# A two-stream transformer layer on one core: norm statistics, delta keys and queries, and triangular blocks of the mixer's front computed in another form

## The chip, the cores and the metric

The kernel runs on one core of a Trainium2 chip. The metric is the device time of one execution in microseconds (us). Five engines of the core work side by side, each through its own queue in a fixed order: PE (matrix products and transposes), DVE (vector operations), ACT (scalar functions, through tables), POOL (vector operations too) and SP (which here only issues DMAs).

## The reference, cut to what matters

One layer over two streams, 1024 latent tokens and 256 context tokens of width 1024, all in fp32: a half step of a gated feed-forward (inner width 2816), a mixer, another half step for the latent tokens, and a last norm. Scales and shifts of the norms come from a conditioning vector through `w_mod`. The mixer has one input projection (`w_in`) and two groups of heads: four of a gated delta rule, run in both directions, and four of attention with norms and rotary embedding.

```python
qkv = silu(centred_dwconv(p[..., :1536], conv_w))            # 5 taps over tokens
q, k, v = split(qkv, 3)
q = l2norm(q per head of 128); k = l2norm(k per head of 128) # x * rsqrt(sum x*x + EPS)
...
kb = k * beta
a_mat = where(strict, (kb @ k^T) * decay, 0)                 # per chunk of 64 tokens
u = triangular_solve(a_mat + eye, v * beta); w = triangular_solve(a_mat + eye, kb * exp(gcum))
...                                                          # scan over chunks: o
out_delta = rmsnorm(o, gain) * silu(z)
aq = rope(rmsnorm(q_attn, q_norm)); ak = rope(rmsnorm(k_attn, k_norm))
```

## The kernel before

Order of the work, with the times at which each part runs in the profiled execution: a start (to 45.6) that turns the context and computes the first modulation columns from `w_mod`; the context loop (to 257.0), eleven steps `g` of up to three products with `ffn_w` in split precision, with side work handed in between by a table (`todo`, L830); the latent half step (a class `HalfStep`, whose steps are drawn from a generator `hs1.stream`); the mixer's second norm with the first projections of v and z (L749, L755); the mixer's front (977.5 to 1424.8); attention together with the delta rule's scan; the output projection, the second half step and the final norm.

In the *front* each projection is a product of the normed activations with a slice of `w_in`, whose fp32 weights are split into a high and a low half (`whi` on ACT, `wlo` on POOL or DVE). Then:

- `conv_head` (L1070) takes a head of k, q or v through five taps. The first tap is on ACT, four are on DVE (`ac<-pp,cols,ac`). Silu is a tanh on ACT and a product on DVE (`ac<-pp,ac`). Then PE transposes `ac` to token rows (L1105) and DVE copies them to `tk` (L1110). For k and q, ACT sums squares, DVE makes a reciprocal root of the sums (`rsq`, L1018: two integer steps, three rounds of three), POOL multiplies `tk` by it, PE transposes back (L1124), ACT copies, and a DMA stores the result in `kT_d` or `qT_d`. It is a generator that stops once, before POOL's product; `pump` and `late` resume it a head later.
- `rope_out` (L1034) does the same for one chunk of 128 tokens and two attention heads: a copy and two sums of squares on ACT, twelve small DVE steps, two DVE products, and for latent chunks four POOL steps.
- `stage1` (L1233) makes the strictly triangular blocks of two directions for one of ten chunks: products on PE into `psD`, an exponential on ACT, masks on POOL, products on DVE (`s1N`), transposes (L1258), stores into `nb_d`.
- `invert` (L1268) inverts the 32x32 diagonal blocks, by forward substitution, in three batches of 128, 128 and 64 blocks, one block per partition: two DVE steps (`tmb`, `Xb`) for each of 31 columns, then a DVE copy `Lb` (L1282) and two stores. Batches follow their chunks: four, four and two calls of `stage1`, then one `invert`.
- The last stage (from about 1366) runs the last 256 columns of the attention's q and of z, chunk by chunk, while `stage2_load` (L1306) has SP read the blocks back into `slot` tiles.

A scheduler sets the order on each engine when the program is built: each engine's queue is fixed, and steps of different places stand interleaved in it, roughly in the order of the program.

## Time and profile before

| | us |
|---|---|
| median of 3 runs | 2517.65 |
| lowest, highest run | 2512.27, 2519.01 |
| profiled execution | 2513.8 |
| its span | 2512.0 |
| busy in it: PE, DVE, ACT, POOL | 2353.8, 1884.6, 1129.3, 879.0 |

The mean granted clock of the profiled execution is 0.975. Over the whole span PE is busy 94% of the time and DVE 75%, but these shares are averages over stages of different kinds. The chain of work that ended last puts 52% of the span on PE and 21% on DVE. So what a change in one stage is worth is read from the table by stretches and from PE's waits in that stretch.

### The profile page before, as it was taken

What the parts mean: (1) busy time and instruction counts of PE and PEld (TensorE: products, weight loads), DVE (VectorE), ACT (ScalarE), POOL (GpSimd) and SP (SyncE); (2) the same over time, 40 slices, a digit from 0 to 9 for tenths busy, and PEclk for the clock granted to TensorE, in tenths of its full rate; (3) what the DMA queues carried; (4) which work ended last, traced back from release to release, by engine and by line L of the source; (5) the groups of instructions that cost most, each with busy time, mean ns of one, the idle gap of its engine ahead of it and who ended that gap; (6) DMA issues with size and microseconds to landing.
All of it is one profiled execution on the core that took longest, in us unless ns stands there. A gap on an engine that the chain in (4) does not pass through costs nothing.

```text
span 2512.0 us, 36679 instructions
## 1 busy us (share of the span) xinstructions
PE 2353.8 (94%) x12877; PEld 2004.7 (80%) x12877; DVE 1884.6 (75%) x3354; ACT 1129.3 (45%) x2355; POOL 879.0 (35%) x734
## 2 busy tenths in 40 slices
PE   8999999999989998988787899998999999999998
PEld 5999887877778878866676799887877888877887
DVE  4779768988798864677999766798488456667886
ACT  4575533332233454354443365566274334223445
POOL 0000243545532333345522534531034444663320
PEclk9999999999999999989898999999999999999999
DMA  8966425465684433324422545532333324446432
GB/s 299 303 205 220 163 101 168 143 209 202 203 278 138 139 134 100 91 60 131 125 83 83 152 115 180 171 101 108 119 101 126 126 106 155 151 160 217 139 126 84
DMA packets 345111, 377.86 MB, mean 150 GB/s; under 512 B 73707, under 2 KB 249503, under 8 KB 344543
## 3 DMA queue, kind: packets, MB, share of 16 engines
q1 hardware_dynamic: 311856, 328.16, 40.3%
q10 hardware_dynamic: 33071, 47.36, 5.8%
q8 instruction: 102, 1.67, 0.3%
q14 instruction: 82, 0.67, 0.1%
HBM read 283.41 MB, written 92.01 MB: 149 GB/s over the span
## 4 chain that ended last, share of the span: by engine, by line
PE 52%; DVE 21%; issue 8%; DMA 7%; POOL 6%; ACT 5%; SPq 1%; ACTq 0%; DVEq 0%; POOLq 0%
PE psw L407 28%; PE pd L55 7%; PE psA L55 6%; DVE ac L52 3%; DVE macc L52 3%; DVE ulo L49 2%; PE psw L55 2%; PE po L55 2%; DMA wr<-in_ffn_w 2%; PE pS L55 1%; DMA R<-gda 1%; PE psB L55 1%; PE psY L860 1%; DVE k L49 1%; DVE tmb L49 1%
## 5 line engine op out<-in xcount | busy, mean ns | idle before, releaser
L407 PE MATMUL psw<-xo,uhi 128*128 128x512 f32 x1536 | 492.7, 398 | 32.2 <-DVE k L49 15.6
L407 PEld LDWEIGHTS psw<-xo,uhi 128*128 128x128 f32 x1536 | 295.5, 192 | 100.0 <-ACT k L46 14.1
L407 PE MATMUL psw<-slot,uhi 128*128 128x512 f32 x1024 | 319.8, 390 | 5.1 <-DVE nk L49 3.0
L407 PE MATMUL psw<-xo,ulo 128*128 128x512 f32 x768 | 304.5, 396 | 0.0
L49 DVE TENSOR_TENSOR ulo<-wr,uhi 128x512 fp32r<-128x512 f32 (+1 forms) x272 | 215.1, 813 | 67.5 <-ACT uhi L46 64.4
L49 POOL TENSOR_TENSOR R<-wr 128x512 f32<-128x512 f32 (+1 forms) x68 | 95.4, 1413 | 391.0 <-DMA wr<-in_ffn_w 348.9
L407 PEld LDWEIGHTS psw<-slot,uhi 128*128 128x128 f32 x1024 | 192.2, 188 | 46.7 <-issue 3.8
L46 ACT ACTIVATE uhi<-wr 128x512 fp32r<-128x512 f32 (+1 forms) x272 | 150.8, 597 | 128.3 <-PE psw L407 68.3
L407 PE MATMUL psw<-slot,ulo 128*128 128x512 f32 x512 | 199.2, 389 | 0.0
L407 PEld LDWEIGHTS psw<-xo,ulo 128*128 128x128 f32 x768 | 148.0, 193 | 30.6
L55 PE MATMUL psA<-hc,whi 128*128 128x256 f32 x832 | 155.7, 285 | 1.8 <-ACT sil L46 1.8
L52 DVE SCALAR_TENSOR_TENSOR macc<-wv,cs,macc 128x512 f32<-128x512 f32 x140 | 135.6, 987 | 17.4 <-DMA wv<-in_w_mod 16.3
L46 ACT ACTIVATE whi<-wr 128x1024 fp32r<-128x1024 f32 x100 | 104.3, 1054 | 98.0 <-PE pd L55 27.4
L49 POOL TENSOR_TENSOR ext<-wr 128x512 f32<-128x512 f32 (+1 forms) x68 | 91.0, 1348 | 151.5 <-DMA wr<-in_ffn_w 150.1
L49 DVE TENSOR_TENSOR ulo<-ext,uhi 128x512 fp32r<-128x512 f32 (+1 forms) x102 | 96.8, 976 | 52.6 <-ACT uhi L46 52.3
L55 PEld LDWEIGHTS psA<-hc,whi 128*128 128x128 f32 x832 | 131.7, 192 | 3.0 <-ACT sil L46 2.0
L49 DVE TENSOR_TENSOR wlo<-wr,whi 128x1024 fp32r<-128x1024 f32 x82 | 100.6, 1238 | 32.5 <-ACT whi L46 32.4
L55 PE MATMUL psA<-hc,wlo 128*128 128x256 f32 x416 | 118.1, 284 | 0.1
L46 ACT ACTIVATE k<-k 128x512 f32<-128x512 f32 x57 | 36.0, 632 | 179.0 <-DVE k L49 179.0
L407 PEld LDWEIGHTS psw<-slot,ulo 128*128 128x128 f32 x512 | 96.1, 188 | 19.8
L49 POOL TENSOR_TENSOR wr<-wr 128x512 f32<-128x512 f32 (+1 forms) x68 | 93.3, 1372 | 45.4 <-DMA wr<-in_ffn_w 38.3
L46 ACT ACTIVATE uhi<-ext 128x512 fp32r<-128x512 f32 (+1 forms) x102 | 57.1, 599 | 110.8 <-POOL ext L49 57.0
(489 smaller groups left out, 6483.6 us busy)
## 6 DMA issues: line engine op xcount, KB each, us to landing
wr<-in_ffn_w SPq DMA_DIRECT2D x174, 512.0 KB, 4.9
wv<-in_w_mod SPq DMA_DIRECT2D x128, 256.0 KB, 3.2
R<-gda ACTq DMA_DIRECT2D x74, 256.0 KB, 3.9
wr<-in_ffn_w SPq DMA_DIRECT2D x32, 384.0 KB, 5.2
...
```

Source lines behind the costliest of these rows:

```text
L46: return nc.scalar.activation(out, in_, func, **kw)
L49: return (eng or nc.vector).tensor_tensor(out=out, in0=a, in1=b, op=op)
L52: return nc.vector.scalar_tensor_tensor(out=out, in0=a, scalar=s, in1=b, op0=op0, op1=op1)
L55: nc.tensor.matmul(out, l, r, start=start, stop=stop)
L407: nc.tensor.matmul(banks[u][key], l[:, u, k, :], r_, start=new and i == 0, stop=i == 3 * pr.kq - 1, skip_group_check=True)
L860: nc.tensor.matmul(Yc[d // 2][:, d % 2 * TC : d % 2 * TC + TC], l, r_, start=g == 0 and i == 0 and d % 2 == 0, stop=g == NF2 - 1 and i == ...
```

## The change

- *Start*: twelve small loads move from ACT's queue to SP's queue, ahead of the modulation weights; the conditioning rows share one tile with the other rows; the context is turned first.
- *Context loop*: the table of side work is one step earlier for the turns; the last W2 split uses a buffer of the pair `w2p`, which the product of step 9 holds until then; a step of `hs1.stream` stands where that split was.
- *Silu* is one function on ACT, for the convs and for z.
- *Delta k and q* stay unscaled. `kT_d` and `qT_d` are stored from `ac` directly. Squares are one ACT step over whole rows, and the norms are products of 128x128 with a column of ones. The scale of k goes into the columns `beta` and `nbeta`; that of q goes into `epsq`, used in the last norm (`gated`). Second transposes and POOL's product are gone; the copies to `tk` are on ACT.
- *Rope* is a class that collects four chunks and makes the statistics of eight heads at once.
- *Triangular blocks*: `stage1` stands chunk by chunk between the chunks of the k projection. The inverse holds all three batches in one tile (62 DVE steps), is a generator that starts after the tenth `stage1`, and advances six columns after each of six conv heads.

```diff
-        nc.scalar.dma_start(cxt[t], A["ctx"][0][t * P : (t + 1) * P, :])
+        xt = wp.tile([P, 1024], F32, tag="raw", name="xt", bufs=2)
+        nc.sync.dma_start(xt, A["ctx"][0][t * P : (t + 1) * P, :])
+        turn_in(xt, xc, t)
...
+    for n, ap in (("c", A["c"][0]), ("c_ctx", A["c_ctx"]), ("g_ffn1", A["g_ffn1"][0]), ("g_mix", A["g_mix"][0]),
+                  ("g_ffn2", A["g_ffn2"][0]), ("b_mod", A["b_mod"][0]), ("g_final", A["g_final"])):
...
+        nc.sync.dma_start(rows1[r : r + k, :], ap.rearrange("(r p) -> r p", p=P))
...
+    nc.sync.dma_start(rows2, A["dn_conv"][0].rearrange("t (r p) -> (t r) p", p=P))
...
+    nc.tensor.transpose(pt[:, 0:P], rows1, ident)
+    nc.vector.tensor_copy(cols1, pt[:, 0:P])
...
+    act(cs[:, :, 0], col1("c"), AF.Silu)
+    act(cs[:, :, 1], col1("c_ctx"), AF.Silu)
...
-    nc.scalar.dma_start(alog, A["dn_a_log"][0].rearrange("d h -> (d h)").partition_broadcast(P))
-    nc.scalar.dma_start(dtb, A["dn_dt_bias"][0].rearrange("d h -> (d h)").partition_broadcast(P))
+    nc.sync.dma_start(alog, A["dn_a_log"][0].rearrange("d h -> (d h)").partition_broadcast(P))
+    nc.sync.dma_start(dtb, A["dn_dt_bias"][0].rearrange("d h -> (d h)").partition_broadcast(P))
...
-        act(th, pa, AF.Tanh, scale=0.5)
-        stt(th, th, 1.0, pa, ALU.add, ALU.mult)
+        act(th, pa, AF.Silu)
...
+    adv(n1, 9)
...
-        mod_chunks((q, 4 + q), modst, other_rows if q == 0 else lambda: None)
+        mod_chunks((q, 4 + q), modst)
...
-        adv(n1, (8, 5, 2, 2)[q])
+        adv(n1, 2)
...
+        0: steps_of(x_load, (0,), (1,)),
+        1: steps_of(lambda t: turn_in(xst[t], xl, t), (0,), (1,)) + steps_of(x_load, (2,), (3,)),
+        2: steps_of(lambda t: turn_in(xst[t], xl, t), (2,), (3,)) + steps_of(x_spill, (0,)) + steps_of(x_load, (4,), (5,)),
+        3: steps_of(lambda t: turn_in(xst[t], xl, t), (4,), (5,)) + steps_of(hs1.squares, *((d, 0, 512) for d in range(8))) + steps_of(x_load, (6,), (7,)),
+        4: steps_of(lambda t: turn_in(xst[t], xl, t), (6,), (7,)) + steps_of(x_spill, (512,)) + more(rest[0], 5),
+        5: more(rest[0], 5) + steps_of(hs1.squares, *((d, 512, 512) for d in range(4))),
...
+    for g in range(3, 10):
+        todo[g] = todo.get(g, []) + more(mc, 3)
...
-            W2_last = split_rows(raw2)
+            next(hs1.stream)
...
-        W2 = split_rows(raw_rows(f2, g * 256), w2p) if g < NF2 - 1 else W2_last
+        W2 = split_rows(raw_rows(f2, g * 256) if g < NF2 - 1 else raw2, w2p)
         prev = g_
-    next(hs1.stream)
     next(hs1.stream)
...
+    adv(n2[512], 2)
...
-    def rope_out(c, pa, gain, dst, d0, rope):
...
+    class Rope:
...
+        def __call__(self, c, pa):
+            b = self.batch[c]
+            n = 2 * len(b)
+            if c == b[0]:
+                self.p = rp.tile([P, 8, P], F32, tag="xr", name="xr", bufs=2)
+                self.ss = const.tile([P, 8], F32, tag="ssc", name="ssc", bufs=2)
+            i = 2 * b.index(c)
+            act(self.p[:, i : i + 2, :], pa.rearrange("p (h e) -> p h e", h=2), AF.Copy)
...
+            for h in range(2):
+                act(junk, self.p[:, i + h, :], AF.Square, accum_out=self.ss[:, i + h : i + h + 1])
+            if c == b[-1]:
+                self.turn(b, n)
+
+        def turn(self, b, n):
+            rs = const.tile([P, 8], F32, tag="rsc", name="rsc", bufs=2)
+            ss = self.ss[:, 0:n]
+            nc.vector.tensor_scalar(out=ss, in0=ss, scalar1=1.0 / P, scalar2=EPS, op0=ALU.mult, op1=ALU.add)
+            rsq(rs[:, 0:n], ss)
+            for i, c in enumerate(b):
+                xn = self.p[:, 2 * i : 2 * i + 2, :]
+                for h in range(2):
...
+                if c < 8:
...
+                    tt(t1, xn, cc[:, 0:1, :].to_broadcast([P, 2, P]), ALU.mult, nc.gpsimd)
...
+                        tt(t2[:, :, :, w], xv[:, :, :, 1 - w], sv[:, :, w].unsqueeze(1).to_broadcast([P, 2, 64]), ALU.mult, nc.gpsimd)
+                    tt(xn, t1, t2.rearrange("p h e w -> p h (e w)"), ALU.add, nc.gpsimd)
+                nc.sync.dma_start(self.dst[c][:, self.d0 : self.d0 + 256], xn.rearrange("p h e -> p (h e)"))
...
+    FOURS = [(0, 1, 2, 3), (4, 5, 6, 7)]
...
-            th = pp[:, po : po + n]
-            act(th, ac[:, t0 : t0 + n], AF.Tanh, scale=0.5)
-            stt(ac[:, t0 : t0 + n], th, 1.0, ac[:, t0 : t0 + n], ALU.add, ALU.mult)
-        groups = [(0, 4), (4, 4)] + ([(8, 2)] if ctx_too else [])
+            act(ac[:, t0 : t0 + n], ac[:, t0 : t0 + n], AF.Silu)
+            if kind != "v":
+                act(pp[:, po : po + n], ac[:, t0 : t0 + n], AF.Square)
+                c0 = t0 // P
+                nc.sync.dma_start((kT_d if kind == "k" else qT_d)[c0 : c0 + n // P, :, h * P : (h + 1) * P].rearrange("c p e -> p c e"),
+                                  ac[:, t0 : t0 + n].rearrange("p (c e) -> p c e", e=P))
+        yield
...
+        if kind != "v":
+            pn = pst("Y")[:, 0:nch]
+            for c in range(nch):
+                o = c * P if c < 8 else LW + c * P - T
+                mm(pn[:, c : c + 1], pp[:, o : o + P], ones[:, 0:1])
+            if kind == "k":
+                act(ssk[:, :, h], pn, AF.Copy)
...
+                nc.vector.tensor_scalar(out=epsq[:, :, h], in0=pn, scalar1=P * EPS, scalar2=P * EPS * EPS, op0=ALU.mult, op1=ALU.add)
...
+            tk = m1.tile([P, NC, P], F32, tag="tk", name="tk", bufs=2)
+            for c0, n in ((0, 4), (4, 4), (8, 2)):
...
-                    act(sq, p3[:, j, :], AF.Square, accum_out=ss[:, c0 + j : c0 + j + 1])
...
-                tt(tk[:, c0 : c0 + n, :], tk[:, c0 : c0 + n, :], rs[:, c0 : c0 + n].unsqueeze(2).to_broadcast([P, n, P]), ALU.mult, nc.gpsimd)
-                pb = pst("Y")
-                for j in range(n):
-                    nc.tensor.transpose(pb[:, j * P : (j + 1) * P], tk[:, c0 + j, :], ident)
-                tb = m1.tile([P, 4, P], F32, tag="tb", name="tb", bufs=2)
-                act(tb[:, :n, :], pb.rearrange("p (c e) -> p c e", c=4)[:, :n, :], AF.Copy)
...
+                    c = c0 + j
+                    nc.tensor.transpose(pt[:, j * P : (j + 1) * P], ac[:, c * P : (c + 1) * P], ident)
+                act(tk[:, c0 : c0 + n, :], pt.rearrange("p (c e) -> p c e", c=4)[:, :n, :], AF.Copy)
...
         W = load_cols(w_in, c0 + pr * 256, spare=True)
         for f in range(2):
             gen = conv_head(kind, pr * 2 + f, W, f)
             next(gen, 0)
             pump()
             late.append(gen)
+            then()
...
+    ssk = smalls[:, 5, 0:40].rearrange("p (c h) -> p c h", h=4)
+    epsq = smalls[:, 5, 40:72].rearrange("p (c h) -> p c h", h=4)
...
-            rope_out(c, pa[:, 16:272], gq, aq_d, 0, True)
+            rope_q(c, pa[:, 16:272])
...
+    flush()
+
+    rk, rt = e1[:, :, 0:4], e1[:, :, 4:8]
+    nc.vector.tensor_scalar_add(ssk, ssk, EPS)
+    rsq(rk, ssk, rt)
+    tt(rt, rk, rk, ALU.mult)
+    for t_, r_ in ((beta, rk), (nbeta, rt)):
+        t4 = t_.rearrange("p c (d h) -> p c d h", d=2)
+        tt(t4, t4, r_.unsqueeze(2).to_broadcast([P, NC, 2, 4]), ALU.mult)
+    tt(nbe, nbeta, egc, ALU.mult)
...
+    def invert():
+        L, X = (m3.tile([P, 3, 32, 32], F32, name=nm) for nm in ("Lb", "Xb"))
+        tm = m3.tile([P, 3 * 272], F32, name="tmb")
+        Lf, Xf = (t.rearrange("p m r q -> p m (r q)") for t in (L, X))
+        nc.gpsimd.memset(Lf[64:128, 2], 0.0)
...
         for k in range(31):
             r, q = 31 - k, k + 1
-            t = tm[0:n, 0 : r * q].rearrange("p (r q) -> p r q", q=q)
...
-        nc.sync.dma_start(xx_d[bi][0:n], Xf[0:n])
-        nc.sync.dma_start(xx_d[bi][n : 2 * n], L[0:n].rearrange("p r q -> p (r q)"))
...
+            t = tm[:, 0 : 3 * r * q].rearrange("p (m r q) -> p m r q", m=3, q=q)
+            tt(t, L[:, :, k + 1 :, k : k + 1].to_broadcast([P, 3, r, q]), X[:, :, k : k + 1, 0:q].to_broadcast([P, 3, r, q]), ALU.mult)
+            tt(X[:, :, k + 1 :, 0:q], X[:, :, k + 1 :, 0:q], t, ALU.add)
+            yield
+        for m in range(3):
+            n = 64 * len(BATCH[m])
+            act(L[0:n, m], X[0:n, m].rearrange("p r q -> p q r"), AF.Copy)
+            nc.sync.dma_start(xx_d[m][0:n], Xf[0:n, m])
+            nc.sync.dma_start(xx_d[m][n : 2 * n], Lf[0:n, m])
+
+    rope_k = Rope(gk, ak_d, 0, FOURS + [(8, 9)])
+    W = load_cols(w_in, 2576, spare=True)
+    for c in range(10):
+        stage1(c // 2, c % 2)
+        rope_k(c, tok_mm(hsel, W, c, 256)[:, 0:256])
+    es_m2.close()
+    m3, es_m3 = open_pool("m3", side="right")
+    inv = invert()
+    next(inv)
     conv_pair("v", 1024, 0)
-    conv_pair("q", 0, 0)
-    conv_pair("q", 0, 1)
-    conv_pair("v", 1024, 1)
-    es_m2.close()
+    for kind, c0, pr in (("q", 0, 0), ("q", 0, 1), ("v", 1024, 1)):
+        conv_pair(kind, c0, pr, lambda: adv(inv, 6))
+    run(inv)
+    es_m3.close()
     es_hc.close()
...
+    rope_q = Rope(gq, aq_d, 256, FOURS)
...
-        rope_out(c, tok_mm(hsel, W[0], c, 256)[:, 0:256], gq, aq_d, 256, True)
+        rope_q(c, tok_mm(hsel, W[0], c, 256)[:, 0:256])
...
-        nc.vector.tensor_scalar(out=ss, in0=ss, scalar1=1.0 / P, scalar2=EPS, op0=ALU.mult, op1=ALU.add)
+        stt(ss, ss, 1.0 / P, epsq[:, c, :], ALU.mult, ALU.add)
```

The queue of DVE at the end of the convs and in the last stage. Names: `tmb`, `Xb` are the inverse, `ac<-pp` conv taps, `kl` attention keys, `ss`, `rs`, `ssc`, `rsc`, `rsq_t` the reciprocal root, `th` the silu of z. First before, then the change.

```order
L1341 MEMSET slot_12504 128x4096
L1341 MEMSET slot_12526 128x4096
L49 TENSOR_TENSOR kl<-psY,kh 128x256
L1042 TENSOR_SCALAR ss<-ss 128x2
L52 SCALAR_TENSOR_TENSOR th<-th,psB 128x256
L1020 TENSOR_SCALAR rs<-ss 128x2
L1021 TENSOR_SCALAR rs<-rs 128x2
L52 SCALAR_TENSOR_TENSOR rsq_t<-rs 128x2
L49 TENSOR_TENSOR rsq_t<-rsq_t,ss 128x2
L52 SCALAR_TENSOR_TENSOR rs<-rsq_t,rs 128x2
```

```order
L49 TENSOR_TENSOR tmb<-Lb,Xb 128x180
L49 TENSOR_TENSOR Xb<-Xb,tmb 128x3x2x30
L49 TENSOR_TENSOR tmb<-Lb,Xb 128x93
L49 TENSOR_TENSOR Xb<-Xb,tmb 128x3x31
L52 SCALAR_TENSOR_TENSOR ac<-pp,cols_203,ac 128x1024 x4
L1344 MEMSET slot_11812 128x4096
L1344 MEMSET slot_11854 128x4096
L49 TENSOR_TENSOR kl<-psY,kh 128x256 x4
L1050 TENSOR_SCALAR ssc<-ssc 128x8
L1012 TENSOR_SCALAR rsc<-ssc 128x8
L1013 TENSOR_SCALAR rsc<-rsc 128x8
L52 SCALAR_TENSOR_TENSOR rsq_t<-rsc 128x8
```

In the change the inverse ends one conv head before the clearing of the slot tiles, the reciprocal roots serve eight heads at once, and the step on `th` is gone.

The queue of SP at the same place. `xx_d` are the stores of the inverse, `z_d`, `vt_d`, `aq_d` stores of z, v and q; the row on `slot` is the first of 30 loads of `stage2_load`. First before, then the change.

```order
L753 DMA z_d_103<-th 128x256
L1130 DMA vt_d<-tk 128x4x128 x2
L1130 DMA vt_d<-tk 128x2x128
L1283 DMA xx_d_102<-Xb 64x1024
L1284 DMA xx_d_102<-Lb 64x1024
L1048 DMA cc<-in_rope 128x2x128
L1057 DMA aq_d_111<-xn 128x256
L753 DMA z_d_104<-th 128x256
L1312 DMA slot_12506<-nt_d_68 32x16x32
```

```order
L1289 DMA xx_d_100<-Lb 128x1024
L1288 DMA xx_d_101<-Xb 128x1024
L1289 DMA xx_d_101<-Lb 128x1024
L1288 DMA xx_d_102<-Xb 64x1024
L1289 DMA xx_d_102<-Lb 64x1024
L1122 DMA vt_d<-tk 128x4x128 x2
L1122 DMA vt_d<-tk 128x2x128
L746 DMA z_d_103<-th 128x256
L746 DMA z_d_104<-th 128x256
L1315 DMA slot_11814<-nt_d_68 32x16x32
```

All stores of the inverse now stand together a few rows ahead of the block of slot loads; before, only those of the third batch did. The block keeps its place behind the store of the fifth chunk of z.

The queue of ACT in stage 1, where `s1E` and `s1gm` are its exponentials, `xr` the copies of rope, `ac` the convs. First before, then the change.

```order
L46 ACTIVATE xr<-psB 128x256
L46 ACTIVATE xn,ss<-xr 128x128 x2
L46 ACTIVATE s1E<-psD 128x512
L46 ACTIVATE s1gm<-masks,g 128x128 x8
L46 ACTIVATE xr<-psB 128x256
L46 ACTIVATE xn,ss<-xr 128x128 x2
L46 ACTIVATE s1NT<-psD 128x512
```

```order
L46 ACTIVATE tk<-psY 128x512 x2
L46 ACT_TABLE_LOAD
L46 ACTIVATE s1E<-psD 128x512
L46 ACTIVATE tk<-psY 128x256
L46 ACTIVATE xr<-psB 128x256
L46 ACTIVATE sq,ssc<-xr 128x128 x2
L46 ACT_TABLE_LOAD
L46 ACTIVATE ac<-ac 128x1024
L46 ACTIVATE xr<-psB 128x256
```

Before, no table load stands in this stretch; in the change a conv's silu next to an exponential brings one on either side.

## Rows read from the trace of the kernel before

**Rows 1.** Engines by stretches: stretch, length, busy us (count) of each, clock, DMA share, GB/s.

```profile
core 0: us, PE busy (x) PEld busy (x) DVE busy (x) ACT busy (x) POOL busy (x), PEclk, DMA share, GB/s
45.60:257.00 211.40, 208.92 (x1699) 205.62 (x1698) 166.66 (x225) 128.90 (x173) 0.21 (x1) 1.00 0.74 245
977.50:1147.50 170.00, 152.42 (x980) 137.22 (x978) 107.53 (x291) 72.84 (x232) 63.22 (x82) 0.95 0.28 84
1147.50:1242.00 94.50, 73.61 (x395) 56.90 (x396) 79.41 (x159) 46.03 (x123) 49.98 (x51) 0.89 0.38 108
1242.00:1365.80 123.80, 102.40 (x493) 85.50 (x491) 116.41 (x245) 53.16 (x132) 38.82 (x38) 0.91 0.30 93
1365.80:1424.80 59.00, 49.45 (x363) 47.37 (x364) 42.17 (x143) 15.28 (x58) 25.05 (x32) 0.93 0.49 118
```

**Rows 2.** PE's waits in the front: tile and line, releaser, us, times, longest.

```profile
PE psY L1105 <- DVE ac L52: 19.2, 7, 4.0
PE psD L1258 <- DVE s1N L49: 18.8, 6, 8.4
PE psB L55 <- DVE th L52: 13.3, 4, 6.2
PE psD L55 <- DVE gs L1205: 7.5, 1, 7.5
...
PE psY L1124 <- POOL tk L49: 1.9, 4, 0.7
```

**Rows 3.** DVE by line in the front: operation, count, busy us, mean ns, idle before.

```profile
L49 DVE TENSOR_TENSOR tmb<-Lb,Xb 128x31 f32<-128x31 f32 (+23 forms) x93 | 44.5, 479 | 5.1 <-DMA Lb<-nb_d 3.7
L49 DVE TENSOR_TENSOR Xb<-Xb,tmb 128x31 f32<-128x31 f32 (+23 forms) x93 | 43.2, 465 | 1.4
L52 DVE SCALAR_TENSOR_TENSOR rs<-rsq_t,rs 128x2 f32<-128x2 f32 x78 | 20.0, 258 | 2.0
...
L52 DVE SCALAR_TENSOR_TENSOR ac<-pp,ac 128x1024 f32<-128x1024 f32 (+1 forms) x20 | 18.4, 927 | 2.1 <-ACT pp L46 2.1
...
L1110 DVE COPY tk<-psY 128x512 f32<-128x512 f32 (+1 forms) x20 | 12.4, 633 | 12.0 <-PE psY L1105 12.0
...
L1042 DVE TENSOR_SCALAR ss<-ss 128x2 f32<-128x2 f32 x26 | 8.9, 342 | 13.5 <-ACT xn L46 13.4
...
L52 DVE SCALAR_TENSOR_TENSOR rsq_t<-rsc 128x10 f32<-128x10 f32 (+1 forms) x24 | 6.1, 254 | 0.2
...
L52 DVE SCALAR_TENSOR_TENSOR th<-th,psB 128x256 f32<-128x256 f32 x12 | 5.0, 416 | 14.6 <-ACT th L46 14.6
```

**Rows 4.** DVE's timeline near 1281: start, us, line, operation.

```profile
1281.02 0.42 DVE L49 TENSOR_TENSOR tmb<-Lb,Xb 128x256 f32<-128x256 f32 x1
...
1283.02 2.62 DVE L49 TENSOR_TENSOR tmb<-Lb,Xb 128x255 f32<-128x255 f32 x1
```

**Rows 5.** POOL's timeline at the same place.

```profile
1282.65 2.70 POOL L49 TENSOR_TENSOR wlo<-wr,whi 128x1024 fp32r<-128x1024 f32 x1 [3.26 <-ACT whi L46]
```

**Rows 6.** POOL by line in the front.

```profile
L49 POOL TENSOR_TENSOR tk<-tk,rsc 128x512 f32<-128x512 f32 (+1 forms) x20 | 25.7, 1308 | 39.6 <-DVE rsc L52 24.4 <-DVE rs L52 15.1
```

**Rows 7.** ACT's timeline around a table load of the front.

```profile
1080.60 0.27 ACT L46 ACTIVATE e<-e 128x80 f32<-128x80 f32 x1
1080.89 1.28 ACT L46 ACT_TABLE_LOAD   x1
1082.18 0.27 ACT L46 ACTIVATE e<-e 128x80 f32<-128x80 f32 x1
```

**Rows 8.** PE's timeline: eight products with one column.

```profile
2484.72 1.05 PE L55 MATMUL psA<-ones,facc 128*128 128x1 f32 x8
```

**Rows 9.** Timeline of the start, SP and PE; a wait stands in brackets.

```profile
0.72 0.41 SPq L131 DMA_DIRECT2D rows<-in_c  x1
...
11.57 2.71 PE L55 MATMUL psY<-ms,cs 128*2 128x256 f32 x8 [2.02 <-ACT cs L46]
```

**Rows 10.** The page's groups by line: the high half of a weight split.

```profile
L46 ACT ACTIVATE whi<-wr 128x1024 fp32r<-128x1024 f32 x100 | 104.3, 1054 | 98.0 <-PE pd L55 27.4
```

**Rows 11.** POOL's timeline: three rope products of one chunk.

```profile
1136.66 2.23 POOL L49 TENSOR_TENSOR t<-xn,cc 128x256 f32<-128x256 f32 x3
```

**Rows 12.** SP's timeline: the last loads of the block of slots.

```profile
1393.52 8.86 SPq L1312 DMA_DIRECT2D slot<-xx_d  x16
```

More of the change, by code (lines that the diff above doesn't have):

```diff
@@ L150, in block_kernel @@
-    act(cs.rearrange("p k b -> p b k"), pt[:, 0:16].rearrange("p (b k) -> p b k", b=2), AF.Silu)
+    nc.tensor.transpose(pt[:, 0:P], rows1, ident)
+    nc.vector.tensor_copy(cols1, pt[:, 0:P])
+    pt = pst("D")
+    nc.tensor.transpose(pt[:, 0:60], rows2, ident[0:60, 0:60])
+    nc.vector.tensor_copy(cols2, pt[:, 0:60])
     def col1(n, k=8):
         return cols1[:, off[n] : off[n] + k]
-    def other_rows():
-        pt = pst("D")
-        nc.tensor.transpose(pt[:, 0:P], rows1, ident)
-        nc.vector.tensor_copy(cols1, pt[:, 0:P])
-        pt = pst("D")
-        nc.tensor.transpose(pt[:, 0:60], rows2, ident[0:60, 0:60])
-        nc.vector.tensor_copy(cols2, pt[:, 0:60])
-        for t in range(2):
-            turn_in(cxt[t], xc, t)
+    cs = const.tile([P, KT, 2], F32, name="cs")
@@ L1128, in conv_head @@
-        if kind != "q":
-            for c0, n in groups:
+            act(ac[:, t0 : t0 + n], ac[:, t0 : t0 + n], AF.Silu)
[5 more added lines that the diff above has]
+        yield
+        nch = 10 if ctx_too else 8
@@ L1130, in conv_head @@
                 nc.sync.dma_start((kt_d if kind == "k" else vt_d)[c0 : c0 + n, :, h * P : (h + 1) * P].rearrange("c p e -> p c e"), tk[:, c0 : c0 + n, :])
-    def conv_kind(kind, c0):
-        for pr in range(2):
-            conv_pair(kind, c0, pr)
     late = []
@@ L1145, in flush, with conv_pair @@
             pump()
-    def conv_pair(kind, c0, pr):
+    def conv_pair(kind, c0, pr, then=lambda: None):
         W = load_cols(w_in, c0 + pr * 256, spare=True)
@@ new lines, in invert @@
+            yield
+        for m in range(3):
+            n = 64 * len(BATCH[m])
+            act(L[0:n, m], X[0:n, m].rearrange("p r q -> p q r"), AF.Copy)
[7 more added lines that the diff above has]
+    es_m2.close()
```

138 lines of the change are left out of this document (31 added, 107 removed).

## The prediction

> **What bounds the kernel now.** I read the engine table by stretches first [rows 1]. In the context loop (45.6 to 257.0) PE is busy 208.92 of 211.40 us at granted clock 1.00: nothing but PE work counts there. The mixer's front, 977.5 to 1424.8, is different: its four stretches hold 447.3 us, and PE is busy 152.42 + 73.61 + 102.40 + 49.45 = 377.9 of them. So PE stands still for about 69 us. It also runs slower: with the two clock levels 1.2 and 2.4 GHz, a mean of 0.95, 0.89, 0.91 and 0.93 means about 2 x (0.05 x 170 + 0.11 x 94.5 + 0.09 x 123.8 + 0.07 x 59) = 68 us at the lower level, in which half, 34 us, is lost to the clock. In the third stretch DVE is busy 116.41 of 123.80 us: DVE, not PE, sets the pace there.
>
> The chain of PE's waits says what PE stands still for [rows 2]: the conv transposes wait for the last DVE step of the conv (19.2 us in 7 waits), stage 1's transposes for its DVE product (18.8 in 6), the projection of the last stage for the gate's step on DVE (13.3 in 4), one block for the log decays (7.5), and the second transposes for POOL (1.9). All but the last are DVE: the DVE queue is late. Whose work makes it late is in the groups by line [rows 3].
>
> **What the change takes from DVE** (345.5 us busy in the front, from rows 1). The rope statistics: six groups of 26 or 78, of which rows 3 hold the first and the last (20.0 and 8.9; together 86.2 us, 3.3 us a call), become 7 batches instead of 26 calls; at the same 3 us a batch that is 20 us, so 66 less. The per-head norms of k and q (seven groups, the first 6.1, together 20.9) become one chain on 40 columns, about 5: 16 less. Silu without its product saves 18.4 + 5.0 = 23.4. The copies of the first transposes go to ACT: 12.4 less (the three copies of the transposed inverse too, not counted here). The inverse is 44.5 + 43.2 = 87.7 us in 186 instructions. A 128x256 step takes 0.42 us [rows 4], small steps about 0.17; that gives 0.17 fixed plus 0.98 ns an element. Both kernels process 3 x 2 x 5456 elements, 32.1 us; 62 instead of 186 fixed parts give 42.6 instead of 63.7 us. The present 87.7 is 24 us above that: the same step takes 2.62 us while POOL's weight split of 2.70 us runs [rows 4, 5]. I leave 15 us of this in: 58, or 30 less. In all 148 us leave DVE, and 198 of 447 remain: DVE no longer sets the pace of the front as a whole.
>
> By the Trainium skill, "SBUF — State Buffer", section "SBUF: two separate sides", VectorE and GpSimd share a port pair under an exclusive lock, which is how rows 4 and 5 read; the wider steps would then be blocked less often, since there are fewer of them.
>
> POOL loses the scaling of k and q, 25.7 us [rows 6]. ACT loses 72 statistics and the copies of the second transposes, and gets squares in whole rows, the copies from DVE and table loads. Before, the front has 2 table loads; the change's order has 11, because Silu, Exp and Copy/Square now alternate (the ACT listing). One load takes 1.28 us, and the next instruction starts right behind it [rows 7]; 9 more are 11.5 us of ACT, with about 187 of 447 us busy [rows 1]: paid only where PE waits for ACT, in stage 1.
>
> By the Trainium skill, "ScalarE: Activation LUTs", section "What ACT_TABLE_LOAD costs", a switch also drains the pipe and takes about 2.66 us. The trace shows no such gap in rows 7; by the page nine loads would cost an estimated 12 us more of ACT, and the sum would be an estimated 2486 instead of 2480.
>
> **The sum**, against the profiled execution of 2513.8 us:
> - *PE's waits in the front.* The conv's last step comes without a product behind it and without rope chains ahead: 19.2 to 4. Stage 1: its POOL steps stay, rope now sends POOL its products four chunks at a time, and the scales of k are a new chain ahead of it: 18.8 to 10. The last stage: no product on DVE, but SP still holds the z store behind the block of slot loads: 13.3 to 7. Log decays 7.5 to 3, second transposes 1.9 to 0. Together -36 (bounds -15: only the product and the transposes; -60: nearly all).
> - *Clock.* It is lower where PE was idle; half the waits go, so I take half of 34: -18 (0 to -34).
> - *New delays.* Table loads ahead of stage 1's exponentials, at most 6 x 1.28 = 8 with the chain of scales: +4 (0 to 12). The inverse now stands between the convs of 1242 to 1365.8: conv steps plus inverse are about 100 us of DVE there, against 102.4 of PE, nearly level: +4 (0 to 25).
> - *PE's own work.* 104 transposes go and 72 norm products of 128x1, two passes each, come. Eight of such take 1.05 us [rows 8], 0.13 each; a transpose is the same. (144 - 104) x 0.13 = +5.
> - *Start.* SP issues 12 small loads ahead of the modulation weights. Before, the first weights' products start at 11.57 us and wait for ACT's conditioning, not for weights [rows 9], and PE is busy from there; the loads cost some 0.4 us of SP each, about 5 us, of which most hides in the wait for the conditioning: +2 (-2 to +15, if the weights run late throughout).
> - *Last W2 split of the context loop.* It can now begin only when the product before it has let its buffer go. One ACT half of it takes 1.05 us, two of them and a DVE half come before PE can start: +4 (0 to 8) [rows 10]. What covers it, 96 products of the half step's stream, is moved into that place, so I take half of the bound.
> - The delta norm, gain and silu of z behind the front: a handful of equal instructions, 0.
>
> -36 - 18 + 4 + 4 + 5 + 2 + 4 = -35, or 2478.8. The profiled execution lies 3.9 us under the median of 2517.65, near the lowest run (2512.27); I add part of this: **2480 us**.
>
> **The rivals.** (A) *PE becomes the bound throughout.* If DVE is far enough ahead everywhere, the waits go to about 10 and the clock returns nearly whole: -59 - 30, plus 5 + 2 + 4 and no new delay, gives -70 to -80, about 2440. For it: 148 us less DVE where 69 us are missing. Against it: stage 1 keeps a chain PE, ACT, DVE, POOL, DVE per chunk, and two thirds of PE's front waits lie where several engines take turns.
>
> (B) *The chain moves to POOL and ACT.* Four chunks of rope give POOL some 12 products and 4 sums in one go (three products take 2.23 us [rows 11], so 8.9 us without the sums), and stage 1's masks queue behind them; the loads come on top. Then stage 1 keeps its 18.8, the convs lose some, the clock stays: -36 becomes -18, -18 becomes -6, new delays +8: about -5 to -15, 2502. For it: POOL is busy 49.98 of 94.5 us in that stretch [rows 1], and its order is fixed. Against it: 26 us of scaling leave POOL.
>
> (C) *The inverse ends too late: slower.* It starts after the tenth chunk of stage 1, not after the fourth, and ends in front of the last conv. Behind it come copies on ACT, six stores, the block of 30 slot loads on SP (its last 16 run from 1393.52 for 8.86 us, to 1402.4 [rows 12]), and then the delta stage, which begins where the front ends, at 1424.8: 22 us of slack. If the strided steps on four axes cost three times what the flat ones do, the inverse is 68 us longer than my 58, and PE stands still for what exceeds the slack and the 20 us the convs leave DVE: 68 - 42 = 26, and convs waiting behind it at the lower clock as much again; against gains of 35 that is about +20 to +30: 2540. It decides from about 1.4 us a step on the mean, against 0.94 forecast. Against it: the rows show about 1 ns an element whatever the shape of the square.
>
> (D) *Table loads that stop ACT for longer than their row.* If ACT also had to run dry at each of the nine more switches, as it would with as much empty time beside each load as its own 1.28 us, ACT would lose 9 x 1.28 = 12 us more, of which six switches' worth, 8 us, lie in stage 1 where PE waits for it: 2480 + 6 to 8, about 2487. Against it: rows 7, where ACT's next instruction starts 0.01 us after the load ends and the one before ended as the load began. The page on ACT named above is the source of that rule.
>
> That the change does not do what it says, or that something at the start costs 30 us, is the rest.
>
> **Chances.** Forecast (2460 to 2500) 0.53; A 0.16; B 0.17; C 0.06; D, whose time lies in the forecast's range, 0.03; rest 0.05. A measurement of this kernel tells about 0.3%, 7.5 us, from no change. Faster: 0.53 + 0.03 + 0.16 + most of B (0.13) = 0.85; same: 0.04 of B and 0.03 of the rest, 0.07; slower: C and the other 0.02, 0.08. The range 2440 to 2508 takes in the forecast, B and the slower half of A; outside lie half of A, C and the rest, 0.19.
>
> **What would show it.** In the changed profile: DVE busy in the front about 190 to 200 us; inverse steps in 62 instructions of up to 1.0 us; the waits of the conv transposes under 5 us; granted clock 0.95 or more; the front some 405 to 415 us long. Wrong if stage 1's transposes still wait 15 us or more, if the first weights' products start after 16 us, if a table load has an empty microsecond behind it, or if the first delta product waits for the slot loads.

## The result and the profile after

The changed kernel takes 2478.14 us (median of 4 runs, 2473.29 to 2482.59), the kernel before 2515.36 in the same comparison: a ratio of 0.9851, 95% interval 0.9826 to 0.9876, some 37 us less. The profiled execution is the slowest of the four, 2482.59 us with a span of 2480.8, 31.2 less than the span before.

The table by stretches, cut in both kernels at the same landmarks: first product of the context loop, first product of the half step, first z and v product of the front, end of stage 1, first product of the last stage, first product of the delta stage, first product of the second half step. The first fence is the kernel before, the second the changed kernel; columns as in [rows 1].

```profile
45.70:314.80 269.10, 266.50 (x1953) 253.38 (x1953) 206.81 (x274) 161.47 (x227) 15.86 (x12) 1.00 0.69 230
...
977.30:1241.30 264.00, 225.53 (x1375) 193.72 (x1374) 186.24 (x446) 118.62 (x354) 113.21 (x132) 0.93 0.32 93
1241.30:1353.60 112.30, 97.03 (x448) 80.35 (x447) 105.19 (x229) 50.10 (x128) 36.19 (x37) 0.91 0.32 98
1353.60:1424.40 70.80, 55.12 (x409) 52.72 (x408) 53.86 (x161) 18.46 (x61) 27.28 (x33) 0.93 0.43 103
1424.40:1846.10 421.70, 400.38 (x2811) 358.43 (x2811) 308.55 (x809) 241.49 (x603) 137.80 (x126) 1.00 0.43 132
```

```profile
48.40:321.70 273.30, 266.37 (x1953) 252.79 (x1953) 209.14 (x275) 163.14 (x227) 16.13 (x11) 0.99 0.70 232
...
985.70:1224.70 239.00, 217.95 (x1390) 191.81 (x1389) 92.44 (x197) 120.38 (x297) 98.61 (x123) 0.95 0.35 105
1224.70:1323.40 98.70, 95.68 (x469) 79.94 (x469) 83.95 (x93) 39.32 (x52) 25.25 (x28) 0.96 0.26 77
1323.40:1386.10 62.70, 54.16 (x414) 52.56 (x412) 26.19 (x53) 26.18 (x67) 19.73 (x20) 0.92 0.57 146
1386.10:1812.50 426.40, 402.07 (x2812) 360.38 (x2811) 312.00 (x816) 243.59 (x605) 145.44 (x138) 0.99 0.43 133
```

The front is 46.7 us shorter (447.1 to 400.4): 25.0 up to the end of stage 1, 13.6 in the convs of v and q, 8.1 in the last stage. DVE is busy 202.6 us in it instead of 345.3. PE's idle time falls from 69.4 to 32.6 us, and its busy time from 377.7 to 367.8, at a higher clock in the first two stretches. The middle stretch is now PE's: 95.68 of 98.70 us. Outside the front it goes the other way: 2.7 us at the start, 4.2 in the context loop, 1.5 in the half step, 4.7 in the delta stage, 2.4 behind it. -46.7 + 2.7 + 4.2 + 1.5 + 4.7 + 2.4 = -31.2, the difference of the spans.

PE's waits in the front of the changed kernel (us in total, times, longest), against [rows 2]:

```profile
PE psD L1258 <- DVE s1N L49: 8.6, 6, 2.4
PE psD L55 <- DVE gs L1197: 5.5, 1, 5.5
PE psB L55 <- ACT whi L46: 4.2, 1, 4.2
PE psD L1258 <- ACT s1gm L46: 4.0, 1, 4.0
PE psD L55 <- ACT s1NT L46: 2.2, 2, 1.6
PE psY L1120 <- ACT tk L46: 1.8, 1, 1.8
```

No wait for the conv's `ac` is left, and none for a gate step on DVE; the conv's transposes (L1120) now wait 1.8 us for ACT's copies. DVE by line in the changed front, against [rows 3]:

```profile
L49 DVE TENSOR_TENSOR tmb<-Lb,Xb 128x93 f32<-128x93 f32 (+15 forms) x31 | 28.3, 914 | 0.5
L49 DVE TENSOR_TENSOR Xb<-Xb,tmb 128x93 f32<-128x93 f32 (+15 forms) x31 | 26.0, 840 | 0.5
...
L52 DVE SCALAR_TENSOR_TENSOR rsc<-rsq_t,rsc 128x8 f32<-128x8 f32 (+1 forms) x21 | 5.4, 259 | 0.6
```

The inverse is 54.3 us in 62 steps, and the rope's roots are in groups of 21 and 7 steps, together 19.6 us. The start and the loop, PE's waits in them:

```profile
PE psA L121 <- DMA xt<-in_ctx: 5.2, 1, 5.2
PE psY L852 <- ACT whi L46: 3.3, 1, 3.3
...
PE psY L852 <- DVE wlo L49: 0.6, 1, 0.6
```

The first row was 2.0 us before. The second and third rows are the last W2 split, 3.9 us that PE did not wait before.

### The profile page after: what moved, and what is told of

Its sections match the earlier page's. It is cut to its first block, busy times and chain, and to the rows that moved or that the text cites. A ratio compares the mean times of both kernels' runs of the same rounds, so it can differ in the third digit from the quotient of the medians.

```text
span 2480.8 us, 36035 instructions
## 1 busy us (share of the span) xinstructions
PE 2349.7 (95%) x12916; PEld 2004.3 (81%) x12916; DVE 1749.3 (71%) x2865; ACT 1135.0 (46%) x2236; POOL 857.0 (35%) x715
## 4 chain that ended last, share of the span: by engine, by line
PE 35%; DVE 7%; ACT 4%; POOL 3%; issue 3%; DMA 2%; SPq 1%; DVEq 0%; ACTq 0%; POOLq 0%
PE psw L401 18%; PE pd L55 6%; PE psA L55 3%; PE psB L55 2%; PE psw L55 2%; PE po L55 1%; PE pS L55 1%; POOL ext L49 1%; PE pt L1611 1%; DVE ac L52 1%; PE psD L55 1%; DMA wr<-in_ffn_w 1%; DVE el L49 1%; SPq L1315 1%; POOL gt L49 1%
## 5 line engine op out<-in xcount | busy, mean ns | idle before, releaser
L401 PEld LDWEIGHTS psw<-xo,uhi 128*128 128x128 f32 x1536 | 293.6, 191 | 99.8 <-ACT k L46 14.8
L401 PE MATMUL psw<-slot,uhi 128*128 128x512 f32 x1024 | 321.7, 392 | 4.2 <-DVE nk L49 3.6
L49 POOL TENSOR_TENSOR R<-wr 128x512 f32<-128x512 f32 (+1 forms) x68 | 97.0, 1436 | 400.9 <-DMA wr<-in_ffn_w 376.6
L55 PE MATMUL psA<-hc,whi 128*128 128x256 f32 x832 | 150.2, 281 | 0.0
L52 DVE SCALAR_TENSOR_TENSOR macc<-wv,cs,macc 128x512 f32<-128x512 f32 x140 | 135.5, 987 | 16.6 <-DMA wv<-in_w_mod 15.2
L52 DVE SCALAR_TENSOR_TENSOR ac<-pp,cols,ac 128x1024 f32<-128x1024 f32 (+1 forms) x80 | 83.2, 1049 | 74.5 <-ACT ac L46 73.5
L49 DVE TENSOR_TENSOR ulo<-ext,uhi 128x512 fp32r<-128x512 f32 (+1 forms) x102 | 97.0, 979 | 54.3 <-ACT uhi L46 53.9
L401 PEld LDWEIGHTS psw<-slot,ulo 128*128 128x128 f32 x512 | 96.6, 189 | 20.3
L49 POOL TENSOR_TENSOR wr<-wr 128x512 f32<-128x512 f32 (+1 forms) x68 | 94.5, 1389 | 47.3 <-DMA wr<-in_ffn_w 37.7
```

Of the source, the lines that this page charges most:

```text
L49: return (eng or nc.vector).tensor_tensor(out=out, in0=a, in1=b, op=op)
L52: return nc.vector.scalar_tensor_tensor(out=out, in0=a, scalar=s, in1=b, op0=op0, op1=op1)
L55: nc.tensor.matmul(out, l, r, start=start, stop=stop)
L401: nc.tensor.matmul(banks[u][key], l[:, u, k, :], r_, start=new and i == 0, stop=i == 3 * pr.kq - 1, skip_group_check=True)
```

## The experiments

All medians below come with the ratio to the kernel before, run beside them; the changed kernel has 0.9851. Two theories stood against each other. **Load**: PE stood still because DVE's queue was late, and the 143 us that left DVE are the gain. **Order**: the gain comes from where transposes and stage 1 now stand. A median carries the whole execution; where a run lost its time is read from its profiled execution, above all from the way from the first product of the front to the first product of the scan (451.2 us in the changed kernel, 494.4 before). A table of it for all runs ends this section.

### Three parts undone, one by one and together

```diff
-    FOURS = [(0, 1, 2, 3), (4, 5, 6, 7)]
+    FOURS = [(c,) for c in range(8)]
-    rope_k = Rope(gk, ak_d, 0, FOURS + [(8, 9)])
+    rope_k = Rope(gk, ak_d, 0, FOURS + [(8,), (9,)])
```

> The changed kernel, with the rope statistics taken chunk by chunk again (26 chains of 12 small DVE steps in place of 7). Theory 1 (load: PE stood still because DVE's queue was late, and the gain comes from the 143 us that left DVE): about 66 us of DVE come back, but into stretches where DVE is now busy 92 of 239 and 26 of 63 us, so most fits: +5 to +15 us on the changed kernel's 2478. Theory 2 (order: the gain comes from the transposes standing a head later and from stage 1 standing between the chunks of k; the DVE work taken away was beside PE anyway): 0 to +3.

Measured: 2501.29 us, 0.9941 (0.9926 to 0.9955), 23 us lost. That is more than either theory said. The largest place is in the timelines of PE and ACT of that run, last stage:

```profile
1377.99 0.58 PE L55 MATMUL psB<-whi,hha 128*128 128x256 f32 x1 [13.18 <-ACT xr L46]
```

```profile
1377.55 0.38 ACT L46 ACTIVATE xr<-psB 128x256 f32<-128x256 f32 x1 [12.32 <-DMA aq_d<-xr]
```

PE waits 13.18 us for a copy on ACT, and that copy 12.32 us for its buffer, whose store stands on SP behind the slot loads. My edit had left two buffers, which now held one chunk each and not four. So the load was tried again with eight (and the tiles of the statistics narrowed to two columns):

```diff
-                self.p = rp.tile([P, 8, P], F32, tag="xr", name="xr", bufs=2)
+                self.p = rp.tile([P, n, P], F32, tag="xr", name="xr", bufs=8)
```

> As rope_by_ones, but with eight buffers of one chunk in place of two (so that as many chunks are in flight as in the changed kernel, in the same memory). In rope_by_ones PE waited 13.2 us at one place of the last stage, where a rope copy on ACT waited for its buffer, whose store stood on SP behind the block of slot loads. Load: the 66 us of DVE are what cost, so it stays at 2495 to 2503. Buffers: that wait goes, and with it most of the 22 us: 2482 to 2488.

Measured: 2484.62, 0.9876 (0.9859 to 0.9894). The buffers are worth some 17 us, by the medians and on the way to the scan (468.4 us with two, 451.4 with eight). What the small DVE steps cost is not clear of zero: the median is 6 us higher, but the interval overlaps that of the changed kernel, and with DVE busy 52 us more in the front (254.5 against 202.6) the way to the scan is only 0.2 us longer. Holding eight chunks, so that no store behind the slot loads stops ACT, is a part of the change that its words don't name. It is not 17 us of the gain, though: the kernel before had three buffers of `xn`, not two.

```diff
-            t = tm[:, 0 : 3 * r * q].rearrange("p (m r q) -> p m r q", m=3, q=q)
...
+            for m in range(3):
+                t = tm[:, 272 * m : 272 * m + r * q].rearrange("p (r q) -> p r q", q=q)
...
```

> The changed kernel, with each of the 62 DVE steps of the inverse issued as three, one per batch, at the same place. Load: 124 more fixed parts of about 0.17 us, 21 us, into the stretch of the convs of v and q, where DVE is busy 84.0 of 98.7 us and PE 95.7: the stretch grows to about 105 to 115, +8 to +15 us in all. Order: the steps stay where they are, 0 to +3.

Measured: 2487.17, 0.9892 (0.9874 to 0.9909): 9 us lost, as load has it in sum, with an interval that just overlaps that of the changed kernel. The trace does not put it down to load: DVE is busy 7.4 us more in the front, the stretch of the convs grew by 1 us (99.8), and the way to the scan by 0.4 (451.6). Most of the 10.9 us by which the profiled execution is longer lies where the two programs are the same: 3.5 in the context loop, 3.4 in the half step, 2.4 behind the scan's first product.

```diff
-            act(ac[:, t0 : t0 + n], ac[:, t0 : t0 + n], AF.Silu)
+            act(th, ac[:, t0 : t0 + n], AF.Tanh, scale=0.5)
+            stt(ac[:, t0 : t0 + n], th, 1.0, ac[:, t0 : t0 + n], ALU.add, ALU.mult)
...
-        act(th, pa, AF.Silu)
+        act(th, pa, AF.Tanh, scale=0.5)
+        stt(th, th, 1.0, pa, ALU.add, ALU.mult)
```

The factors that belong to this form come back with it, among them a DVE step that halves the gain `gdn` of the delta norm once it is loaded.

> The changed kernel, with silu as tanh on ACT and a product on DVE, for the convs and z. DVE gets about 23 us back, 11 of them in the stretch of the convs of v and q, and a step more lies between the last tap and the transposes; 12 table loads (15 us of ACT) go. Load: +3 to +10 us, less what the loads give back. Order: within 3 us, or faster by up to 5 if the loads cost something.

Measured: 2502.36, 0.9949 (0.9935 to 0.9962): 24 us lost, far over both. Both theories missed: DVE is busy 30 us more in the front and the way to the scan is 16.6 us longer, where 52 us of DVE had cost 0.2. Of the loss, 10 us lie in the last stage. So z alone was tried (the second half of the diff, with the step on `gdn`):

> The changed kernel, with silu by tanh and a product on DVE for z alone (20 products of 0.42 us, 8 of them in the last stage); the convs keep silu, and the table loads stay. silu_by_tanh cost 24 us, of which 10 were in the last stage, 5 in the convs of v and q and 3 ahead. Load on DVE's total: 8 us of DVE in stretches with room, 0 to +4. Place: the product stands on DVE behind what waits there (slot clears of 3.5 us each, keys, inverse), and the next product of PE needs its PSUM buffer: +8 to +12.

Measured: 2488.47, 0.9902 (0.9883 to 0.9922), 10 to 13 us lost with DVE busy 9 us more in the front: the place decides. The last stage grew by 7.6 us (70.3), the delta stage ahead of the scan by 2.6. The timelines of DVE and of PE there:

```profile
1385.76 3.67 DVE L52 SCALAR_TENSOR_TENSOR xr<-xr,rsc,gq 128x128 f32<-128x128 f32 x8
1389.36 0.41 DVE L52 SCALAR_TENSOR_TENSOR th<-th,psB 128x256 f32<-128x256 f32 x1
...
1403.09 0.23 DVE L1419 TENSOR_SCALAR gdn<-gdn 128x128 f32<-128x128 f32 x1 [6.04 <-DMA gdn<-in_dn_norm]
```

```profile
1389.82 0.51 PE L1568 MATMUL pt<-ident,ldq 128*128 128x128 f32 x2 [4.71 <-DVE th L52]
1405.23 0.79 PE L55 MATMUL pS<-kh,qh 128*128 128x512 f32 x1 [6.00 <-ACT e L46]
```

The last product of z, 0.41 us, reads PE's result and so frees the bank (the memory that PE's products go to) that attention's first transposes need. It stands behind a batch of rope, and PE waits 4.7 us; at an earlier product PE waits 2.9. The step on `gdn` waits 6.0 us for its load with the attention's steps behind it on DVE, and ACT and then PE wait as long. The two clears of `slot` (3.47 us each) also stand ahead of a product here, but no product of PE waits for that one; in the kernel before, PE waited 3.7 us at that place.

All three edits together (rope with two buffers):

> The three edits together: about 110 us of the DVE work that the change took away is back, in the change's order. Load: +25 to +40, that is 2503 to 2518, with the waits of PE for DVE back near 60 us in the front and the granted clock down to about 0.92 there. Order: under +10.

Measured: 2511.57, 0.9985 (0.9974 to 0.9996): 33 of 37 us are gone although order, norms as products and the missing second transposes stay. It isn't load alone that took them: the two buffers are in it, and PE's largest wait in its front is 16.7 us for rope's copies on ACT (0.5 in the changed kernel). The same with eight buffers was not run. The convs and the last stage of that run by stretches:

```profile
1226.70:1331.40 104.70, 98.33 (x494) 82.58 (x493) 97.87 (x193) 40.11 (x54) 20.71 (x29) 0.97 0.27 83
1331.40:1418.60 87.20, 56.98 (x419) 54.54 (x417) 54.25 (x181) 27.01 (x68) 28.27 (x33) 0.86 0.44 114
```

The last stage is 24.5 us longer than in the changed kernel. PE is idle for 30 of its 87 us, and its granted clock is 0.86; in the convs, 6 us longer, PE is idle for 6 of 105 and has 0.97. The single losses (23 + 9 + 24) add up to 56, so they overlap.

### Order, in both kernels

```diff
-        yield
         nch = 10 if ctx_too else 8
...
                 nc.sync.dma_start((kt_d if kind == "k" else vt_d)[c0 : c0 + n, :, h * P : (h + 1) * P].rearrange("c p e -> p c e"), tk[:, c0 : c0 + n, :])
+        yield
```

> The changed kernel, with the norm products and transposes of a conv head right after it, not a head later. Load: DVE is early enough, so PE waits only for the last tap, silu and squares of each head, where the scheduler places other products first: 0 to +8. Order: the waits of the conv transposes come back, near the 19 us of before: +15 to +25.

Measured: 2488.87, 0.9898 (0.9881 to 0.9915), 11 us lost, between the two; the way to the scan is 7.1 us longer. The waits of the transposes did not come back (1.3 us for ACT's `ac`); PE waits 8.3 us for rope's copies on ACT instead. Then the reverse in the kernel before (a `yield` ahead of its first transposes):

> The kernel before, with the first transposes of each conv head a head later (one stop more in its generator), nothing else. Order: the 19.2 us of waits of these transposes go, as transposes_at_once cost 10.7 us in the changed kernel: 2501 to 2508. Load: DVE's queue is as late as before, and PE waits at the next place that needs it: within 4 us of 2516.

Measured: 2511.99, 0.9999 (0.9986 to 1.0013): nothing. Its executions spread from 2503 to 2519, and the profiled one is the lowest, so lengths in its trace say little; the waits say where the time went:

```profile
PE psY L1125 <- POOL tk L49: 20.9, 12, 6.6
PE psD L1259 <- DVE s1N L49: 19.5, 9, 4.5
PE psB L55 <- DVE th L52: 13.3, 6, 8.3
```

The 19.2 us for the first transposes are gone, and the second transposes, which waited 1.9 for POOL, wait 20.9. Likewise the largest single load, alone in the kernel before:

> The kernel before, with the rope statistics alone taken by fours (two buffers of eight heads, the tables in two buffers and not three): 66 us of DVE less, nothing else of the change. Load: in the kernel before DVE is the queue that is late, so the same 66 us that cost 6.5 us in the changed kernel are worth more here, 12 to 25 us: 2491 to 2504. Order: the transposes still stand where they stood, so 0 to 8: 2508 to 2516.

Its edit is the class `Rope` in place of `rope_out`, with two buffers instead of three for the tables and two instead of four for other small tiles of the front (`t1`, `tv`, `kr`). Measured: 2512.26, 0.9993 (0.9982 to 1.0004): nothing, with DVE busy 53 us less in the front and the way to the scan as long as before (494.6 and 494.4). Load alone falls with it, unless the fewer buffers took back what it gave, which was not tried. Its first delta product came 6.7 us earlier (1417.7 against 1424.4), yet the second half step began 2.1 us later: the delta stage up to the scan took 5.4 us more.

### Start, and stores on another queue

The start, the table of side work and the W2 split were put back together:

> The changed kernel, with the start, the table of side work and the last W2 split of the kernel before. In the changed profile the first product of the context loop came at 48.4 us (before 45.7), and the loop up to the half step's first product took 273.3 us (before 269.1), with PE waiting 3.9 us for the split. If these terms are what I took them for (a cost at the start, a wait for the split), both go back: 45.7 and 269, and 2478 becomes about 2471. Rival: the half step is paced by its weights' DMAs, and what is won ahead of it is given back there: 2476 to 2479.

Measured: 2475.27, 0.9837 (0.9818 to 0.9857). The interval overlaps that of the changed kernel, so that it beats it is likely, not shown. The trace has the first loop product at 46.8 (48.4), the half step at 318.3 (321.7): about half of the 7 us. Over all runs the two kinds of loop differ by more: it takes 271.8 to 276.8 us in the eight profiles with the changed start and split, 268.9 to 271.5 in the six with the old ones, 5.7 us on the mean.

```diff
-        rope_out(c, tok_mm(hsel, W[0], c, 256)[:, 0:256], gq, aq_d, 256, True)
-        z_out(c, tok_mm(hsel, W[1], c, 256)[:, 0:256], 256)
+        rope_out(c, tok_mm(hsel, W[0], c, 256)[:, 0:256], gq, aq_d, 256, True, nc.scalar)
+        z_out(c, tok_mm(hsel, W[1], c, 256)[:, 0:256], 256, None, nc.scalar)
```

The new last argument is the queue that issues the store; only the last stage uses ACT's.

> The kernel before, with the stores of q and z of the last stage issued by ACT and not by SP, so that they don't stand behind the block of 30 slot loads. The 13.3 us that PE waits there are put down to DVE's gate step. Load: DVE is late by itself, and the wait stays: within 3 us of 2516. Buffers: the gate step waits for a buffer whose store stands behind the block; the wait goes and the last stage gets 8 to 12 us shorter: 2504 to 2509.

Measured: 2526.8, 1.0046 (1.0031 to 1.0062): 11 us slower, and the wait for the gate step is still 13.8. So the slot loads weren't its cause in the kernel before, DVE was: its timeline has the third batch of the inverse and conv taps ahead of the longest one. The loss shows on ACT, POOL and SP, first in their timelines, then in SP's waits:

```profile
1419.97 0.38 ACT L46 ACTIVATE xr<-psB 128x256 f32<-128x256 f32 x1 [9.59 <-POOL xn L49]
...
1417.10 1.66 POOL L49 TENSOR_TENSOR t<-xn,cc 128x256 f32<-128x256 f32 x3 [15.62 <-DMA cc<-in_rope]
...
1398.09 16.61 SPq L1312 DMA_DIRECT2D slot<-xx_d  x16
1414.80 4.35 SPq L1048 DMA_DIRECT2D cc<-in_rope  x4
```

```profile
SPq L1312 <- DMA aq_d<-xn: 14.6, 3, 6.0
...
SPq L1312 <- DMA z_d<-th: 5.7, 3, 3.7
```

The store of `xn` now stands in ACT's queue, and what is behind it, a copy that frees a bank, waits 9.59 us for POOL. POOL waits 15.62 us for a table of rope (`cc`), whose load stands on SP behind the block of slot loads, and that block takes 16.61 us instead of 8.86 [rows 12]: it now waits for the stores that were moved; in the kernel before no wait of SP's was for a store of q or z. With z alone moved, on top of the changed kernel with the old start:

> As start_and_split_as_before, with the last stage's stores of z issued by ACT, directly behind ACT's own silu, and not by SP behind the block of slot loads (the stores of q stay on SP: on ACT they had to wait for POOL and cost 11 us in before_stores_on_ACT_queue). In the changed profile ACT's silu of z stands 5.7 us for its buffer's store. If that holds PE up: 3 to 5 us less than 2475. If PE waits for something else there: within 2 us of 2475.

Measured: 2482.51, 0.9877 (0.9858 to 0.9895): 7 to 10 us slower, where I expected a gain. The first delta product did come earlier (1375.9, against 1386.1), and it did not help. The tile view of `pd` for the changed kernel and for this run (last columns: first and last start): the first product of the delta stage, and the first of the scan over chunks.

```profile
L55 PE MATMUL pd<-slot,slot x160: 272/275/377, 1386.1 to 1534.9; 128*128 128x128 f32 x160
...
L55 PE MATMUL pd<-dl_S,dl_kT x144: 270/275/275, 1436.9 to 1672.7; 128*128 128x128 f32 x144
```

```profile
L55 PE MATMUL pd<-slot,slot x160: 275/275/377, 1375.9 to 1546.9; 128*128 128x128 f32 x160
...
L55 PE MATMUL pd<-dl_S,dl_kT x144: 270/275/275, 1438.6 to 1672.9; 128*128 128x128 f32 x144
```

From the same views of all runs, in us of one profiled execution each:

| | front to scan | delta stage to scan | scan to second half step |
|---|---|---|---|
| changed | 451.2 | 50.8 | 375.6 |
| rope by ones | 468.4 | 49.9 | 374.7 |
| rope by ones, eight buffers | 451.4 | 50.3 | 376.6 |
| inverse by threes | 451.6 | 49.9 | 378.0 |
| silu by tanh | 467.8 | 49.5 | 379.0 |
| z by tanh | 461.5 | 53.4 | 379.3 |
| all three back | 478.4 | 47.4 | 375.1 |
| transposes at once | 458.3 | 50.0 | 374.2 |
| start and split as before | 450.6 | 50.4 | 375.5 |
| start before, z stores on ACT | 456.8 | 62.7 | 374.7 |
| before | 494.4 | 47.3 | 374.4 |
| before, rope by fours | 494.6 | 52.7 | 377.8 |
| before, transposes later | 490.8 | 47.6 | 374.7 |
| before, stores on ACT | 500.8 | 47.4 | 375.0 |

What lies behind the scan's first product takes 374 to 379 us in all runs. An earlier front counts only as far as the scan starts earlier. In the run with z's stores on ACT that gain was lost in between: PE is busy there for 50.5 of 62.7 us at a granted clock of 0.89 (44.9 of 50.8 at 0.97 in the changed kernel, with the same 320 products), and the scheduler has put the delta stage's next products behind the attention's. SP's timeline, first the changed kernel, then z on ACT, and SP's wait in the latter:

```profile
1360.26 10.49 SPq L1315 DMA_DIRECT2D slot<-xx_d  x16
...
1400.33 0.90 SPq L1412 DMA_DIRECT2D dl_kT<-kT_d  x2
```

```profile
1352.55 30.88 SPq L1323 DMA_DIRECT2D slot<-xx_d  x16
...
1419.04 0.91 SPq L1420 DMA_DIRECT2D dl_kT<-kT_d  x2
```

```profile
SPq L1323 <- DMA z_d<-th: 23.0, 4, 9.6
```

The last sixteen slot loads take 30.88 us in SP's queue instead of 10.49, and the scan's own loads, which stand behind them, come 19 us later. SP's waits say why the block got longer: as in the run above, the slot loads wait for the moved stores, 23.0 us in all. Why a load waits for a store that it doesn't read isn't settled, and neither is how much of the later scan these loads make: no product of PE in that stretch waits for a load.

## Why the prediction was right, and where not

The time (2480 predicted, 2478.14 measured) and the sign were right, and most terms of the sum hold.

- *DVE's own numbers* hold: 198 predicted for the front, 202.6 measured; rope 20 and 19.6; inverse 58 and 54.3. It is 11.7 above the unblocked 42.6, where I had left 15: five of its steps take 2.5 to 3.1 us, each beside a weight split on POOL, as in [rows 4, 5]. By the Trainium skill, "SBUF — State Buffer", section "SBUF: two separate sides", VectorE and GpSimd hold a port pair by turns; that agrees with each of these steps. That wider steps would be blocked less often, as I had read from it, did not come: five steps took over 2 us before as well.
- *Start* +2: 2.7. *W2 split* +4: 4.2, with 3.9 of waits at that place; both by the mechanism named. What stood in its place hid nothing of the split, and over all runs the loop's term is nearer 6.
- *The front as a whole*, -36 - 18 + 4 + 4 + 5 = -41: -46.7. PE's idle time fell by 36.8, against -36 with +8 of new delays. The conv transposes wait 1.8 for ACT (predicted 4), the gate 0.9 for ACT (7), stage 1 8.6 for DVE and 6.2 for ACT (10 and 4), the log decays 5.5 (3). The delay by the one-piece inverse, +4, did not come where it was expected: PE is busy 97% of that stretch. The inverse's copies, left out of the sum, do delay PE behind it: three of them hold ACT for 5.9 us, the next weight split stands behind them, and PE waits 4.2 for `whi`.
- *Clock* -18 and *PE's work* +5, together -13: busy time fell by 9.9, at 0.95, 0.96 and 0.92.
- *Behind the front* I had 0. The delta stage took 4.7 us more, 3.5 of them before the scan. This was the missed term: I treated the front's end as the place where the gain is banked, and it is the scan's start. The half step's 1.5 and the end's 2.4 are within what single runs differ by (661 to 667 us for the half step with the same program).
- *Luck* is in how near the total came: the front gave 5.7 us more than its terms, and 8.6 us behind and ahead of it (4.7 + 1.5 + 2.4) were in no term.

What failed, though the sum stood, is the reasoning behind the first term: that DVE is late because it is loaded, so that 148 us less on it would take most of PE's waits away. The runs show other things in its place. The largest single load, taken away alone in the kernel before (53 us less on DVE), is worth nothing; a later transpose alone is worth nothing there either, for PE then waits at the next place. Put back into the changed kernel, that load (52 us) costs 0.2 us on the way to the scan. What costs time there are places: two buffers instead of eight 17 us, z's products with their step on `gdn` 10, the transposes without a head between 7.

The rivals: A (PE the bound throughout, 10 us of waits) held only in the convs; 32.6 us of idle time remained. B (POOL's rope batches ahead of stage 1's masks) came in one place only: POOL's order has the masks between the chunks, and stage 1's transposes wait 13.0 us in all, 18.8 before. The 4.0 us that are put down to ACT's `s1gm` are that place; the mask `s1B` stands on POOL behind rope's products, and ACT waits for it:

```profile
1153.16 1.26 POOL L49 TENSOR_TENSOR s1B<-s1B,s1gm 128x512 f32<-128x512 f32 x1
...
1154.45 1.28 ACT L46 ACTIVATE s1gm<-masks,g 128x128 f32<-128x128 f32 x4 [5.00 <-POOL s1B L49]
```

C (an inverse that ends too late) did not come: 0.88 us a step on the mean against its point of 1.4, last store of the inverse on SP at 1333.48, delta stage at 1386.1, and no product of the delta stage waits for a slot load. D (table loads that cost twice) shows no sign; ACT's timeline in stage 1:

```profile
1122.51 1.28 ACT L46 ACT_TABLE_LOAD   x1
1123.81 1.06 ACT L46 ACTIVATE ac<-ac 128x1024 f32<-128x1024 f32 x1
```

The next instruction starts 0.02 us after the load. By the Trainium skill, "ScalarE: Activation LUTs", section "What ACT_TABLE_LOAD costs", a drain would come on top; the trace has none here. That silu by tanh, which takes 12 of the program's loads away, was slower by 24 us says that the trade was right; it doesn't price the loads.

What stays open: which part brought how much of the 37 us. The norms as products and the missing second transposes were not undone alone, and the three edits were not run together with eight buffers. With the three back 4 us of gain remain in the median; on the way to the scan 27 of the 43 us are lost and 16 remain.
